# A hybrid decoder block on one core: small products in one run, the first norm from rows of x, x in four-tile pieces, its weights first, the last tile in pieces

## The chip, the core and the metric

The kernel runs on one core of one Trainium2 chip. Its engines are TensorE (PE; PEld is its weight load), VectorE (DVE), ScalarE (ACT), GpSimd (POOL) and SyncE (SP), and each works through its own list of instructions in order. DMAs are issued by an instruction of SP or of ACT. The metric is the device time of one launch in microseconds (us), the median of three runs.

## The reference, cut to what matters

One decoder layer over 256 tokens of width 2048, all in float32:

```python
h = rmsnorm(x, attn_norm_w)                      # x * rsqrt(mean(x*x) + EPS) * w
proj = h @ w_in                                  # 2048 -> 4*1024 + 3*1024 + 2*2048
rq, rk, rv, rg, mq, mk, mv, g_ret, g_moba = split(proj)
o_ret = silu(rg) * groupnorm(retention(rotary(rq), rotary(rk), rv)) * ret_norm_w   # 4 heads of 256
o_moba = causal softmax attention(rotary(mq), rotary(mk), mv)  # 8 heads of 128; 256 tokens are one block
merged = sigmoid(g_ret) * (o_ret @ w_ret_up) + sigmoid(g_moba) * (o_moba @ w_moba_up)
x = x + merged @ w_out
h2 = rmsnorm(x, ffn_norm_w)
a, b = split(causal_dwconv(h2 @ w_ffn_up, conv_w, conv_b))    # 2048 -> 2 * 5632
x = x + (silu(a) * b) @ w_ffn_down                            # 5632 -> 2048
return rmsnorm(x, final_norm_w)
```

## The kernel before

All weights stand in device memory as one stream of *halves*: a half is a tile of 128 x 1024 floats (512 KB), two k tiles (of 128 rows) by 512 columns. Two halves make a *slot*; a *group* is 512 columns of a product, and a group over 2048 rows takes four slots. `plan` lists the groups: values, then keys and queries of the MoBA heads, the same of the retention heads, gates, up-projections, `w_out`, then the feed-forward. Groups of keys and queries use weights as the stationary operand and products of 128x256; values, gates and most others have tokens stationary and products of 128x512.

Every float32 operand is split into a high and a low part: ACT copies `raw` to `whi` (line 131), DVE subtracts to get `wlo` (line 132), and `mm3` (line 142) makes three products, high by high, high by low, low by high. So a half can be multiplied by high parts alone when `whi` is there, and its second product needs `wlo`. `part(n)` splits half n, frees its raw buffer and loads half n + 4 (four raw buffers, four pairs of split buffers). `split2` with a scale (lines 134 and 135) does the same for a k tile of x: `xh` and `xl` in `xb`, times the norm's weight of that row, which lies in `vec`. The other factor of the first norm, r1 = rsqrt(mean of x squared), is the same for a whole token and is multiplied in after the products.

The set-up loads x transposed (`xT`, 16 k tiles of 128 x 256, two in a DMA) through four buffers, alternating with halves on SP's list. `part_x` (line 244) splits two k tiles at a time and, one step behind, squares the two before them on ACT (`sq`, `sqk`, lines 255 and 258) and adds them up on POOL (line 259). `setup` (line 263) is a task: with each slot it goes on to its next `yield`. It loads the constants, sums the squares over partitions by small products with a column of ones (`ss`, line 283), takes the root (POOL, line 186), spreads r1 over partitions (`across`) and scales the rotation tables with it.

Other tasks (one per head or group, started by `closed`) do attention, retention, gates, residuals and activations in stages, one stage a slot: a stage's ACT and DVE work stands behind the splits of the next slot's halves. Their small products on PE (`s`, `pt`, `o` of MoBA, `rs`, `ro`, `tr` of retention, `ftr` transposes) go into a list `between`; the slot's main products (`acc`) go into `stream`. `issue` (line 150) puts them on PE's list: main products in order, and from a third of the slot on, small ones spread evenly among them.

The last slot and the one before it run token tile by token tile, and `finish` (line 512) ends each: the residual is added (DVE, 518), squared with its sum (ACT, 519), the four partial sums are added (520), the root is taken (184, 186), the last 512 columns are multiplied by the final weight (522), and four pieces of 512 columns are scaled and stored, even ones by DVE and SP, odd ones by ACT and its own DMA queue.

Of the kernel before, what the change touches and what calls it, by code (L numbers as in the profile page):

```python
# [17 lines left out]
P = 128  # L18
# [62 lines left out]
def block(ctx: ExitStack, tc: tile.TileContext, a):  # L81
# [21 lines left out]
    n_halves = wts.shape[0]  # L103

    def spans(n):
        step = CW if n < 2 else 2 * CW
        return [slice(c, c + step) for c in range(0, 2 * CW, step)]

    def load(n, *some):
# [39 lines left out]

    def issue():  # L150

        n, m = len(stream), len(between)
        first, done = n // 3, 0
        for i, one_mm in enumerate(stream):
            one_mm()
            while done < m and done * (n - first) < (i + 1 - first) * m:
                between[done]()
                done += 1
        assert done == m
        stream.clear()  # L160
        between.clear()

# [50 lines left out]
                tasks.remove(g)  # L213

    vec = sb.tile([P, NVEC], F32, name="vec")
    nc.scalar.dma_start(vec[:, :V_RET], a["vec"][:, :V_RET])
    ident = sb.tile([P, P], F32, name="ident")
    one = sb.tile([P, 1], F32, name="one")
    nc.gpsimd.memset(one, 1.0)
# [11 lines left out]

    xts = {}

    def load_x(k):
        xts[k] = p0.tile([P, 2, S], F32, name="xt", bufs=RAW_BUFS)
        if k:
            nc.sync.dma_start(xts[k], a["xT"][:, k:k + 2, :])  # L237
            load(k // 2) if k < 2 * RAW_BUFS else None
        else:
            for j in range(2):  # L240
                nc.sync.dma_start(xts[0][:, j, :], a["xT"][:, j, :])
                load(0, spans(0)[j])

    def part_x(k):
        if k < KD:
            for j in range(2):
                split2(xh[:, k + j, :], xl[:, k + j, :], xts[k][:, j, :], vec[:, V_ATTN + k + j:V_ATTN + k + j + 1])
                if k == 0:
                    part(0, spans(0)[j])
        k -= 2  # L250
        if 0 <= k < KD:
            t = xts.pop(k)
            if k == 0:
                k1["sq"] = p0.tile([P, 2, S], F32, name="sq")
                nc.scalar.activation(k1["sq"], t, AF.Square)
            else:
# [3 lines left out]
            if k + 2 * RAW_BUFS < KD:  # L260
                load_x(k + 2 * RAW_BUFS)

    def setup():

        yield
        cst = {}
        nc.sync.dma_start(ident, a["ident"])
        for name, p in (("mask", P), ("rcos", P), ("rsin", P), ("mcos", P), ("msin", 32)):
            cst[name] = p0.tile([p, a[name].shape[1]], F32, name=name)
            nc.sync.dma_start(cst[name], a[name])  # L270
        k1["decay"] = p1.tile([P, RH, S], F32, name="decay")
        nc.sync.dma_start(k1["decay"], a["decay"])
        nc.sync.dma_start(vec[:, V_RET:], a["vec"][:, V_RET:])
        yield
        yield
        yield
        for name, src in (("one", ident), ("mask", cst["mask"])):
            k1[name] = p1.tile([P, P], BF16, name=name + "b")
            nc.scalar.activation(k1[name], src, AF.Copy)
# [4 lines left out]
        yield  # L284
# [9 lines left out]
        nc.vector.tensor_mul(k1["rsin"][:, 1, :], cst["rsin"], b)  # L294

    def keep_v(acc, vh, vl):
        for t in range(NT):
# [213 lines left out]

    def finish(acc, t):

        c = D // CW - 1
        w = slice(c * CW, (c + 1) * CW)
        x3 = big["x2"][:, t, :]
        ss = sb.tile([P, 1], F32, name="ss3t", bufs=2)
        nc.vector.tensor_add(x3[:, w], acc, x3[:, w])
        nc.scalar.activation(acc, x3[:, w], AF.Square, accum_out=big["ss3"][:, t, c:c + 1])
        nc.vector.reduce_sum(ss, big["ss3"][:, t, :], axis=AX.X)  # L520
        r = rsqrt("r3", ss, D)
        nc.vector.tensor_mul(x3[:, w], x3[:, w], big["wf"][:, w])
        for c in range(D // CW):
            w = slice(c * CW, (c + 1) * CW)
            if c % 2:
                nc.scalar.activation(x3[:, w], x3[:, w], AF.Copy, scale=r)  # L526
                nc.scalar.dma_start(orows[:, t, w], x3[:, w])
            else:
                nc.vector.tensor_scalar_mul(x3[:, w], x3[:, w], r)
                nc.sync.dma_start(orows[:, t, w], x3[:, w])  # L530


    now = {}
# [32 lines left out]
    def closed(kind, n, acc, more):  # L566
# [17 lines left out]
        elif kind == "wo":  # L584
            if n == 0:
                assert not tasks, len(tasks)
                right.close()
                pr = pool(right, "pr", "right")
                big["x2"] = pr.tile([P, NT, D], F32, name="x2")
                for k in ("ss2", "ss3"):  # L590
                    big[k] = sb.tile([P, NT, 4], F32, name=k)
# [24 lines left out]
    for n in range(RAW_BUFS):  # L616
        load_x(2 * n)
# [136 lines left out]
```

## Time and profile before

| | |
|---|---|
| median of three runs | 1456.74 us (1455.98 to 1457.03) |
| profiled execution, its own time | 1456.43 us |
| its span, first to last instruction | 1454.6 us |
| PE busy | 1440.2 us, 99% of the span |
| DVE, ACT, POOL busy | 895.2, 708.1, 58.9 us |
| mean granted TensorE clock | 0.998 of full speed |
| moved by DMA | 274.19 MB, mean 188 GB/s |

A row of a timeline reads: start, duration, engine, line, operation, tile written and tiles read, count; in brackets, how long the engine had been idle and what ended that. Rows of one kind that follow each other are merged, and "x2" then spans both. The chain of waits follows the end of the program back to its beginning: at each step to what released it. A window's row gives busy time and count for each engine, then granted clock, busy share of the DMA engines and GB/s.

### The profile page before, as it was taken

How to read it: one execution, taken by the hardware profiler on the slowest of the kernel's cores; microseconds unless marked ns; L12 is line 12 of the kernel's file. 1: busy time of each engine (PE TensorE's matmuls, PEld its weight loads, DVE VectorE, ACT ScalarE, POOL GpSimd, SP SyncE). 2: the span in 40 equal slices, each digit the busy share in tenths (PEclk: the TensorE clock that was granted, in tenths of full speed). 3: DMA queues.
4: the chain of work that ended last, by engine and by line, in shares of the span. 5: the costliest groups of instructions: out<-in, count | busy, mean ns of one | idle time of the engine just before them, and what ended most of it. 6: DMA issues, size and time to landing. Idle time of an engine off the chain costs nothing.

```text
span 1454.6 us, 20207 instructions
## 1 busy us (share of the span) xinstructions
PE 1440.2 (99%) x7910; PEld 1247.0 (86%) x7910; DVE 895.2 (62%) x1114; ACT 708.1 (49%) x933; POOL 58.9 (4%) x45
## 2 busy tenths in 40 slices
PE   8999999999999999999999999999999999999997
PEld 6989889899888888888898888888888888888886
DVE  7666655656554545455567777777777776445453
ACT  6444453444444444444455555555555555444343
POOL 3120200101000000000000000000000000000000
PEclk9999999999999999999999999999999999999999
DMA  8654545555555555566655555555555556555553
GB/s 281 203 174 160 166 162 182 175 186 172 175 188 189 189 191 188 198 217 192 201 188 188 188 189 189 189 188 189 188 189 188 188 189 217 195 195 190 195 194 116
DMA packets 77840, 274.19 MB, mean 188 GB/s; under 512 B 8720, under 2 KB 9776, under 8 KB 77616
## 3 DMA queue, kind: packets, MB, share of 16 engines
q1 hardware_dynamic: 77024, 271.84, 57.3%
q8 instruction: 62, 1.02, 0.3%
q10 hardware_dynamic: 720, 1.06, 0.2%
q14 instruction: 34, 0.28, 0.1%
HBM read 270.77 MB, written 2.10 MB: 188 GB/s over the span
## 4 chain that ended last, share of the span: by engine, by line
PE 97%; issue 1%; DVE 1%; DMA 1%; SPq 0%; ACT 0%; POOLq 0%; POOL 0%; ACTq 0%; DVEq 0%
PE acc L140 95%; DMA raw<-in_wts 1%; PE ftr L148 0%; PE s L140 0%; DVE xb L135 0%; PE o L140 0%; PE rs L140 0%; PE ro L140 0%; DVE wlo L132 0%; PE pt L148 0%; SPq L114 0%; PE tr L148 0%; ACT x L526 0%; SPq L237 0%; POOLq L750 0%
## 5 line engine op out<-in xcount | busy, mean ns | idle before, releaser
L132 DVE TENSOR_TENSOR wlo<-raw,whi 128x1024 fp32r<-128x1024 f32 (+1 forms) x506 | 625.9, 1238 | 526.6 <-ACT whi L131 525.8
L131 ACT ACTIVATE whi<-raw 128x1024 fp32r<-128x1024 f32 (+1 forms) x506 | 534.2, 1057 | 701.6 <-PE acc L140 594.5
L140 PE MATMUL acc<-xb,whi 128*128 128x512 f32 (+1 forms) x2496 | 551.3, 343 | 0.0
L140 PEld LDWEIGHTS acc<-xb,whi 128*128 128x128 f32 x2496 | 423.1, 190 | 43.5
L140 PE MATMUL acc<-xb,wlo 128*128 128x256 f32 x1920 | 352.1, 283 | 0.0
L140 PEld LDWEIGHTS acc<-xb,wlo 128*128 128x128 f32 x1920 | 293.6, 191 | 13.1
L140 PE MATMUL acc<-whi,xb 128*128 128x512 f32 x896 | 289.2, 397 | 0.5 <-ACT whi L131 0.4
L140 PEld LDWEIGHTS acc<-whi,xb 128*128 128x128 f32 x896 | 164.5, 188 | 34.9 <-ACT whi L131 1.6
L140 PE MATMUL acc<-wlo,xb 128*128 128x512 f32 x448 | 177.9, 397 | 3.5 <-DVE wlo L132 3.5
L140 PEld LDWEIGHTS acc<-wlo,xb 128*128 128x128 f32 x448 | 84.2, 188 | 23.0 <-DVE wlo L132 6.5
L140 PE MATMUL acc<-whi,gh 128*128 128x512 f32 x224 | 87.1, 389 | 0.0
L140 PE MATMUL acc<-wlo,gh 128*128 128x512 f32 x224 | 87.1, 389 | 0.0
L140 PE MATMUL acc<-whi,gl 128*128 128x512 f32 x224 | 87.1, 389 | 0.0
L494 DVE SCALAR_TENSOR_TENSOR y<-u,vec,y 128x256 f32<-128x256 f32 x176 | 73.3, 479 | 0.0
L140 PE MATMUL acc<-whi,mgh 128*128 128x512 f32 x128 | 50.9, 398 | 0.0
L140 PE MATMUL acc<-whi,mgl 128*128 128x512 f32 x128 | 50.9, 397 | 0.0
L140 PE MATMUL acc<-wlo,mgh 128*128 128x512 f32 x128 | 50.6, 395 | 0.0
L140 PE MATMUL acc<-whi,otmh 128*128 128x512 f32 x128 | 50.0, 391 | 0.0
L140 PE MATMUL acc<-whi,otml 128*128 128x512 f32 x128 | 49.9, 390 | 0.0
L140 PE MATMUL acc<-wlo,otmh 128*128 128x512 f32 x128 | 49.9, 390 | 0.0
L140 PE MATMUL acc<-whi,otrh 128*128 128x512 f32 x128 | 49.8, 389 | 0.0
L140 PE MATMUL acc<-wlo,otrh 128*128 128x512 f32 x128 | 49.8, 389 | 0.0
(157 smaller groups left out, 1028.7 us busy)
## 6 DMA issues: line engine op xcount, KB each, us to landing
raw<-in_wts SPq DMA_DIRECT2D x502, 512.0 KB, 4.0
xp<-in_x SPq DMA_DIRECT2D x4, 512.0 KB, 6.5
xt<-in_xT SPq DMA_DIRECT2D x7, 256.0 KB, 5.7
raw<-in_wts SPq DMA_DIRECT2D x4, 256.0 KB, 4.4
wf<-in_wf SPq DMA_DIRECT2D x1, 1024.0 KB, 8.1
out<-x SPq DMA_DIRECT2D x4, 256.0 KB, 3.1
out<-x ACTq DMA_DIRECT2D x4, 256.0 KB, 3.3
decay<-in_decay SPq DMA_DIRECT2D x1, 512.0 KB, 4.9
```

The source lines that it names most:

```text
L131: nc.scalar.activation(hi, full, AF.Copy)
L132: nc.vector.tensor_sub(lo, full, f32(hi))
L140: to.append(lambda: nc.tensor.matmul(out, a, b, **kw))
L494: nc.vector.scalar_tensor_tensor(y[:, j, :], u[:, j, i:i + S], cv[j][:, i:i + 1], y[:, j, :], op0=OP.mult, op1=OP.add)
```

## The change

There are five edits, and the code that goes with them.

1. `issue` puts all small products of a slot in one run at the middle of the slot's main products.
2. The first norm's sums come from x in rows (256 tokens by 2048): four tiles of 128 x 1024 are loaded on ACT's queue into the buffers that held the transposed x, squared on ACT with their sums, and added on DVE. The squares of the transposed tiles, POOL's sums and the `ss` products are gone. The stages of `setup` are spread over more slots, and its constants come later.
3. x lies in four buffers of four k tiles, all of it at once: two DMAs of 256 KB, then three of 512 KB. Half 1 comes whole and not in two pieces.
4. The norm's weights come on ACT's queue before anything else there (as before, though now in the code behind the idle products); a copy of one element makes ACT load its table at once.
5. `finish` takes the partial sums of the first three column groups ahead of the end, adds and squares the last 512 columns in two pieces of 256, and stores 3 x 448 columns by DVE and SP and 704 by ACT.

```diff
     def spans(n):
-        step = CW if n < 2 else 2 * CW
+        step = CW if n < 1 else 2 * CW
...
     def issue():
-        n, m = len(stream), len(between)
-        first, done = n // 3, 0
-        for i, one_mm in enumerate(stream):
+        middle = len(stream) // 2
+        for one_mm in stream[:middle] + between + stream[middle:]:
             one_mm()
-            while done < m and done * (n - first) < (i + 1 - first) * m:
-                between[done]()
-                done += 1
...
+    def load_x(k, n=4):
+        if k % 4 == 0:
+            xts[k // 4] = p0.tile([P, 4, S], F32, name="xt", bufs=4)
+        nc.sync.dma_start(xts[k // 4][:, k % 4:k % 4 + n, :], a["xT"][:, k:k + n, :])
     def part_x(k):
+        for j in range(k, min(k + 2, KD)):
+            split2(xh[:, j, :], xl[:, j, :], xts[j // 4][:, j % 4, :], vec[:, V_ATTN + j:V_ATTN + j + 1])
             if k == 0:
-                k1["sq"] = p0.tile([P, 2, S], F32, name="sq")
-                nc.scalar.activation(k1["sq"], t, AF.Square)
-            else:
-                sq = p1.tile([P, 2, S], F32, name="sqk", tag="full", bufs=2)
-                nc.scalar.activation(sq, t, AF.Square)
-                nc.gpsimd.tensor_add(k1["sq"], k1["sq"], sq)
+                part(0, spans(0)[j])
     def setup():
...
+        yield
+        yield
+        yield
+        sums = p0.tile([P, NT, 2], F32, name="sums")
+        rows = []
+        for i in range(4):
+            rows.append(p0.tile([P, D // 2], F32, name="rows", tag="xt", bufs=4))
+            nc.scalar.dma_start(rows[i], xrows[:, i // 2, (i % 2) * D // 2:(i % 2 + 1) * D // 2])
         nc.sync.dma_start(ident, a["ident"])
+        fetch("mask")
+        yield
+        fetch("rcos", "rsin", "mcos", "msin")
+        yield
...
-        ss = att("ss")
-        for t in range(NT):
-            for i in range(2):
-                mm(ss[:, t:t + 1], k1["sq"][:, i, t * P:(t + 1) * P], one, start=i == 0, stop=i == 1)
-        yield
-        k1["r1"] = rsqrt("r1", ss[:, :NT], D)
+        for i in range(4):
+            nc.scalar.activation(rows[i], rows[i], AF.Square, accum_out=sums[:, i // 2, i % 2:i % 2 + 1])
+            if i == 1:
+                yield
+        ss = p0.tile([P, NT], F32, name="ss")
+        nc.vector.reduce_sum(ss, sums, axis=AX.X)
+        k1["r1"] = rsqrt("r1", ss, D)
         yield
         b = across(k1["r1"])
...
     def finish(acc, t):
...
+        nc.vector.reduce_sum(ms[:, 2:], big["ss3"][:, t, :c], axis=AX.X)
+        nc.vector.tensor_scalar(ms[:, 0:1], ms[:, 2:], 1.0 / D, EPS, op0=OP.mult, op1=OP.add)
+        for i, v in enumerate(pieces):
+            nc.vector.tensor_add(x3[:, v], acc[:, i * half:(i + 1) * half], x3[:, v])
+        for i, v in enumerate(pieces):
+            sq = sb.tile([P, half], F32, name="sq3", bufs=2)
+            nc.scalar.activation(sq, x3[:, v], AF.Square, accum_out=big["ss3"][:, t, c + i:c + i + 1])
+            nc.vector.scalar_tensor_tensor(ms[:, i + 1:i + 2], big["ss3"][:, t, c + i:c + i + 1], 1.0 / D,
+                                           ms[:, i:i + 1], op0=OP.mult, op1=OP.add)
+        nc.gpsimd.tensor_tensor(r, ms[:, 2:], mhalf[:, :1], op=OP.pow)
         nc.vector.tensor_mul(x3[:, w], x3[:, w], big["wf"][:, w])
+        step = 448
+        for b in range(0, 3 * step, step):
+            w = slice(b, b + step)
+            nc.vector.tensor_scalar_mul(x3[:, w], x3[:, w], r)
+            nc.sync.dma_start(orows[:, t, w], x3[:, w])
+        w = slice(3 * step, D)
+        nc.scalar.activation(x3[:, w], x3[:, w], AF.Copy, scale=r)
+        nc.scalar.dma_start(orows[:, t, w], x3[:, w])
...
+    nc.scalar.dma_start(vec[:, :V_RET], a["vec"][:, :V_RET])
+    nc.scalar.activation(early, early, AF.Copy)
+    load_x(0, 2)
+    load(0)
+    load_x(2, 2)
+    load(1)
+    load_x(4)
+    load(2)
+    load(3)
+    load_x(8)
     part_x(0)
     part_x(2)
     part(1)
+    load_x(12)
     spawn(setup)
```

What moves can be seen on three stretches of the engines' lists. First, ACT at the start of the program, before (the splits of x, `xb`, and of the halves, `whi`, with the squares between them):

```order
L134 ACT_TABLE_LOAD
L134 ACTIVATE xb<-xt,vec 128x256
L131 ACTIVATE whi<-raw 128x512
L134 ACTIVATE xb<-xt,vec 128x256 x2
L255 ACTIVATE sq<-xt 128x512
L131 ACTIVATE whi<-raw 128x512 x2
L134 ACTIVATE xb<-xt,vec 128x256 x2
L258 ACTIVATE sqk<-xt 128x512
L131 ACTIVATE whi<-raw 128x1024
```

and the same stretch now:

```order
L616 ACT_TABLE_LOAD
L616 ACTIVATE early<-early 128x1
L134 ACTIVATE xb<-xt,vec 128x256
L131 ACTIVATE whi<-raw 128x512
L134 ACTIVATE xb<-xt,vec 128x256 x2
L131 ACTIVATE whi<-raw 128x1024
```

The squares between the splits are gone, and half 1 is split in one instruction. Second, ACT now in slots 3 to 7, where the rows of x are loaded and squared (`rows`, with `sums`), and the values' split `vh` takes r1 as its scale:

```order
L257 DMA rows<-in_x 128x1024 x4
L131 ACTIVATE whi<-raw 128x1024 x4
L265 ACTIVATE oneb<-ident 128x128
L265 ACTIVATE maskb<-mask 128x128
L267 ACTIVATE rows,sums<-rows 128x1024 x2
L131 ACTIVATE whi<-raw 128x1024 x2
L267 ACTIVATE rows,sums<-rows 128x1024 x2
L134 ACTIVATE vh<-acc,r_475 128x512 x2
L131 ACTIVATE whi<-raw 128x1024 x6
```

Before, only the two copies and four `whi` stood between the set-up and `vh`; the four squares have moved here from the first slots, and the second pair stands right ahead of the first reader of r1. Third, PE in slot 10, the first with the scores `s` of a MoBA head, before:

```order
L140 MATMUL s<-mh 128x128
L140 MATMUL acc<-xb,wlo 128x256
L140 MATMUL acc<-xb,whi 128x256 x2
L140 MATMUL acc<-xb,wlo 128x256
L140 MATMUL s<-ml,mh 128x128
L140 MATMUL acc<-xb,whi 128x256 x2
L140 MATMUL acc<-xb,wlo 128x256
L140 MATMUL acc<-xb,whi 128x256
L140 MATMUL s<-mh,ml 128x128
```

and now:

```order
L140 MATMUL acc<-xb,wlo 128x256
L140 MATMUL s<-mh 128x128
L140 MATMUL s<-ml,mh 128x128
L140 MATMUL s<-mh,ml 128x128
L140 LDWEIGHTS oneb
L140 MATMUL s<-maskb,oneb 128x128
L140 MATMUL s<-mh 128x256
L140 MATMUL s<-ml,mh 128x256
L140 MATMUL s<-mh,ml 128x256
L140 MATMUL acc<-xb,whi 128x256 x2
```

The eight products of the head now stand behind each other, with main products only ahead of the run and behind it. In the whole program 304 small products stand in 40 runs: 135 of 128 columns and 75 of 256 in 27 runs among main products of 512 columns, 61 and 33 in 13 runs among main products of 256.

## Rows read from the trace of the kernel before

**Rows 1.** The chain of waits, whole program: start, duration, what, count.

```profile
5.56 7.97 DMA raw<-in_wts
...
50.62 21.12 PE acc L140 x176
...
500.60 62.13 PE acc L140 x274
...
729.18 710.79 PE acc L140 x3783
```

**Rows 2.** Windows for products into `acc` alone, from the first to the 97th.

```profile
5.44:33.70 28.26, 24.61 (x97) 17.58 (x97) 0.00 (x0) 0.00 (x0) 1.00 0.84 292
```

**Rows 3.** Timeline of PE in the first stage.

```profile
14.23 0.50 PE L140 MATMUL acc<-wlo,xb 128*128 128x512 f32 x1 [1.01 <-DVE wlo L132]
...
28.33 0.50 PE L140 MATMUL acc<-wlo,xb 128*128 128x512 f32 x1 [1.00 <-DVE wlo L132]
```

**Rows 4.** Timeline of DVE in the first stage.

```profile
18.97 1.21 DVE L132 TENSOR_TENSOR wlo<-raw,whi 128x1024 fp32r<-128x1024 f32 x1
20.11 1.91 DVE L135 SCALAR_TENSOR_TENSOR xb<-xt,vec,xb 128x256 fp32r<-128x256 f32 x2
21.94 2.32 DVE L132 TENSOR_TENSOR wlo<-raw,whi 128x1024 fp32r<-128x1024 f32 x1
...
28.20 0.87 DVE L135 SCALAR_TENSOR_TENSOR xb<-xt,vec,xb 128x256 fp32r<-128x256 f32 x2
```

**Rows 5.** Timeline of POOL in the first stage.

```profile
21.61 1.57 POOL L259 TENSOR_TENSOR sq<-sq,sqk 128x512 f32<-128x512 f32 x1 [0.27 <-ACT sqk L258]
```

**Rows 6.** Timeline of ACT at the start.

```profile
6.37 0.63 ACT L131 ACTIVATE whi<-raw 128x512 fp32r<-128x512 f32 x1 [0.58 <-DMA raw<-in_wts]
...
10.30 0.91 ACT L134 ACTIVATE xb<-xt,vec 128x256 fp32r<-128x256 f32 x2 [0.77 <-DMA xt<-in_xT]
...
13.90 1.04 ACT L131 ACTIVATE whi<-raw 128x1024 fp32r<-128x1024 f32 x1
```

**Rows 7.** Windows of the first 14 us, all engines.

```profile
0.00:5.60 5.60, 4.01 (x11) 3.02 (x11) 0.94 (x3) 2.52 (x4) 0.34 (x6) 1.00 0.59 187
5.60:9.00 3.40, 3.18 (x12) 1.93 (x12) 2.39 (x5) 2.77 (x7) 0.00 (x0) 1.00 0.95 288
9.00:14.00 5.00, 3.88 (x14) 2.36 (x13) 3.47 (x5) 4.23 (x10) 1.29 (x1) 1.00 1.03 410
```

**Rows 8.** Timeline of ACT in slot 6.

```profile
49.16 0.69 ACT L134 ACTIVATE vh<-acc,r 128x512 fp32r<-128x512 f32 x1 [1.38 <-DVE vl L135]
```

**Rows 9.** The chain of waits from 35 to 75 us.

```profile
35.89 0.12 PE ss L140 x2
36.01 1.06 PE acc L140 x8
...
71.73 0.06 PE s L140
71.79 0.53 PE acc L140 x4
```

**Rows 10.** The chain of waits from 425 to 440 us.

```profile
430.21 0.11 PE ftr L148
...
434.34 5.68 PE acc L140 x25
```

**Rows 11.** Timeline of all engines behind the last product.

```profile
1446.17 0.60 ACT L519 ACTIVATE acc<-x 128x512 f32<-128x512 f32 x1 [1.43 <-DVE x L518]
...
1447.34 0.93 POOL L186 TENSOR_TENSOR r<-r3ms,mhalf 128x1 f32<-128x1 f32 x1 [4.51 <-DVE r3ms L184]
...
1448.31 0.88 DVE L529 TENSOR_SCALAR x<-x,r 128x512 f32<-128x512 f32 x2 [0.45 <-POOL r L186]
1448.82 0.81 SPq L530 DMA_DIRECT2D out<-x  x2
```

**Rows 12.** Windows at the end, all engines.

```profile
1450.00:1452.00 2.00, 0.00 (x0) 0.00 (x0) 0.00 (x0) 0.17 (x1) 0.00 (x0) 0.50 1.07 342
```

More of the change, by code (lines that the diff above doesn't have):

```diff
@@ L215, in block @@
     vec = sb.tile([P, NVEC], F32, name="vec")
-    nc.scalar.dma_start(vec[:, :V_RET], a["vec"][:, :V_RET])
     ident = sb.tile([P, P], F32, name="ident")
-    one = sb.tile([P, 1], F32, name="one")
-    nc.gpsimd.memset(one, 1.0)
+    early = sb.tile([P, 1], F32, name="early")
+    nc.gpsimd.memset(early, 1.0)
     mhalf = sb.tile([P, NT], F32, name="mhalf")
@@ L232, in block, with fetch @@
     xts = {}
[L234 to L238, printed above, removed]
-        else:
-            for j in range(2):
-                nc.sync.dma_start(xts[0][:, j, :], a["xT"][:, j, :])
-                load(0, spans(0)[j])
-    def part_x(k):
[L245 to L252, printed above, removed]
-            if k == 0:
-                k1["sq"] = p0.tile([P, 2, S], F32, name="sq")
-                nc.scalar.activation(k1["sq"], t, AF.Square)
-            else:
-                sq = p1.tile([P, 2, S], F32, name="sqk", tag="full", bufs=2)
-                nc.scalar.activation(sq, t, AF.Square)
-                nc.gpsimd.tensor_add(k1["sq"], k1["sq"], sq)
-            if k + 2 * RAW_BUFS < KD:
-                load_x(k + 2 * RAW_BUFS)
+    def load_x(k, n=4):
+        if k % 4 == 0:
+            xts[k // 4] = p0.tile([P, 4, S], F32, name="xt", bufs=4)
+        nc.sync.dma_start(xts[k // 4][:, k % 4:k % 4 + n, :], a["xT"][:, k:k + n, :])
+    def part_x(k):
+        for j in range(k, min(k + 2, KD)):
+            split2(xh[:, j, :], xl[:, j, :], xts[j // 4][:, j % 4, :], vec[:, V_ATTN + j:V_ATTN + j + 1])
+            if k == 0:
+                part(0, spans(0)[j])
     def setup():
-        yield
         cst = {}
[L267 to L273, printed above, removed]
+        def fetch(*names):
+            for name in names:
+                p = a[name].shape[0]
+                cst[name] = p0.tile([p, a[name].shape[1]], F32, name=name)
+                nc.sync.dma_start(cst[name], a[name])
         yield
@@ L276, in setup @@
         yield
[L277 to L285 removed]
+        sums = p0.tile([P, NT, 2], F32, name="sums")
[3 more added lines that the diff above has]
+            nc.scalar.dma_start(rows[i], xrows[:, i // 2, (i % 2) * D // 2:(i % 2 + 1) * D // 2])
+        nc.sync.dma_start(ident, a["ident"])
+        fetch("mask")
+        yield
+        fetch("rcos", "rsin", "mcos", "msin")
+        yield
+        for name, source in (("one", ident), ("mask", cst["mask"])):
+            k1[name] = p1.tile([P, P], BF16, name=name + "b")
+            nc.scalar.activation(k1[name], source, AF.Copy)
+        for i in range(4):
[5 more added lines that the diff above has]
+        k1["r1"] = rsqrt("r1", ss, D)
         yield
@@ L294, in setup @@
         nc.vector.tensor_mul(k1["rsin"][:, 1, :], cst["rsin"], b)
+        yield
+        k1["decay"] = p1.tile([P, RH, S], F32, name="decay")
+        nc.sync.dma_start(k1["decay"], a["decay"])
+        nc.sync.dma_start(vec[:, V_RET:], a["vec"][:, V_RET:])
     def keep_v(acc, vh, vl):
@@ L512, in finish @@
     def finish(acc, t):
-        c = D // CW - 1
+        c, half = D // CW - 1, CW // 2
         w = slice(c * CW, (c + 1) * CW)
         x3 = big["x2"][:, t, :]
[L517 to L521, printed above, removed]
-        nc.vector.tensor_mul(x3[:, w], x3[:, w], big["wf"][:, w])
[L523 to L530, printed above, removed]
+        ms = sb.tile([P, 3], F32, name="r3ms", bufs=2)
+        r = sb.tile([P, 1], F32, name="r3", bufs=2)
+        nc.vector.reduce_sum(ms[:, 2:], big["ss3"][:, t, :c], axis=AX.X)
+        nc.vector.tensor_scalar(ms[:, 0:1], ms[:, 2:], 1.0 / D, EPS, op0=OP.mult, op1=OP.add)
+        pieces = [slice(c * CW + i * half, c * CW + (i + 1) * half) for i in range(2)]
+        for i, v in enumerate(pieces):
[6 more added lines that the diff above has]
+        nc.gpsimd.tensor_tensor(r, ms[:, 2:], mhalf[:, :1], op=OP.pow)
+        nc.vector.tensor_mul(x3[:, w], x3[:, w], big["wf"][:, w])
+        step = 448
[6 more added lines that the diff above has]
+        nc.scalar.dma_start(orows[:, t, w], x3[:, w])
     now = {}
@@ L590, in closed @@
                 for k in ("ss2", "ss3"):
-                    big[k] = sb.tile([P, NT, 4], F32, name=k)
+                    big[k] = sb.tile([P, NT, 4 + (k == "ss3")], F32, name=k)
             spawn(residual, acc, now["xp"], n)
@@ L614, in block @@
         nc.tensor.matmul(t[:, :S], idle[:, 0, :P], idle[:, 0, :], start=True, stop=True)
-    for n in range(RAW_BUFS):
-        load_x(2 * n)
+    nc.scalar.dma_start(vec[:, :V_RET], a["vec"][:, :V_RET])
[8 more added lines that the diff above has]
+    load_x(8)
     part_x(0)
```

1 line of the change is left out of this document (removed).

## Prediction

> **What bounds the kernel now.** I read the chain of waits first. It is PE nearly all the way: from 729 us to 1440 us one unbroken line of main products, before that main products with small ones between them, and in front of all that a stretch of DMA, DVE and ACT [rows 1]. So there are only three places where time can be won: the first stage, the small products, and what follows the last product. A product of 512 columns costs 62.13/274 = 0.2268 us in that line and one of 256 columns 21.12/176 = 0.12 us [rows 1].
>
> The windows on `acc` give the first stage its size. Its 96 products (the row counts the next one too) run from 5.44 to 33.70 us, 28.26 us, where 96 x 0.2268 = 21.8 would do [rows 2]. So 6.5 us are stops. The PE timeline names them: a second product of a half waits about 1 us for DVE's `wlo`, first at 14.23, last at 28.33 [rows 3]. DVE's own timeline shows why: where POOL is idle a `wlo` takes 1.21 and the low parts of two k tiles 0.87; beside POOL's addition of squares, such as the one at 21.61, they take 2.32 and 1.91 [rows 4, 5]. The undisturbed work of a half is 1.21 + 0.87 = 2.08 us on DVE and 1.04 + 0.91 = 1.95 on ACT [rows 4, 6], both under the 12 x 0.2268 = 2.72 that PE needs; disturbed it is over that.
>
> **Transposed squares out, x in four tiles, half 1 whole (edits 2 to 4, first stage).** With POOL's seven additions gone nothing in DVE's way is left, and behind the opening PE should run without a stop. The opening is set by the DMAs. The windows give about 1.05 MB moved by 5.6 us, then 288 GB/s to 9 us and 410 to 14 us [rows 7]. Against them I lay three landings. The second piece of half 0 is the 0.79th MB in SP's order and would be through at about 4.7; ACT had it at 6.37. The tiles of x for half 2 are the 1.84th MB, 8.3 by the windows, and ACT had them at 10.30 [rows 6]. Half 3 is the 3.15th MB, 11.7 by the windows, and landed at 5.56 + 7.97 = 13.53 [rows 1]. So a piece lands 1.7 to 2.0 us after its last byte's turn in issue order.
>
> In the new order x tiles 0 and 1, half 0, x tiles 2 and 3 are again the first 1.05 MB, done at 5.6. Half 1 follows, 0.52 MB: through at 6.9 (at 410 GB/s) or 7.4 (at 288), landed at 8.7 to 9.3. It is now one ACT instruction of 1.04 and one DVE instruction of 1.21, so its second product comes at about 11.1 to 11.7, later than in two pieces. Eleven more products (2.5 us) bring PE to 13.6 to 14.2. Half 2 has 0.52 MB of x and itself ahead: through at 9.5 to 11, landed at 11.3 to 12.9, its `wlo` done 2.25 later, at 13.6 to 15.2. So the second product of half 2, at 14.23 before, stands between 13.6 and 15.2. I take 14.1, since x now also comes in pieces of 4 KB per partition as the stretch with 410 GB/s mostly had them. From there 71 products at 0.2268 make 16.1 us: the stage ends at 30.2 instead of 33.70, a gain of 3.5 (2.4 to 4.0 by the two ends). That ACT loads its table early, and that the first piece of x is twice as large, moves the first product by some tenths and nothing behind half 1.
>
> The `ss` products: two passes take 0.12, and eight main products behind them 1.06 instead of 0.96, so each costs 0.22 [rows 9]; four are gone: 0.9.
>
> What comes instead is four loads of 512 KB on ACT's queue in slot 3 and four squares of 128x1024 in slots 5 and 6, which I put at 1.04 to 1.3 each from the split of that size [rows 6]. They cost nothing as long as ACT and DVE stay ahead of PE. Slot 3 begins at about 24.8; 2.1 MB take 5 us at 410 GB/s plus 2 to land, so the rows are there by 34 or 35, and the first square, behind slot 5's splits, is not due before 37. The narrow place is slot 6. PE enters it at 30.2 + 2 x 48 x 0.12 = 41.7. ACT then splits its second half until 42.8, squares until 45.3; DVE's sums 0.3 and POOL's root 0.93 [rows 11] give r1 at 46.6; behind it stand `vh` 0.69, a wait of 1.38 for DVE and `vh` again [rows 8], to 49.4, and only then the split of slot 8's first half, whose low part is ready at about 51.7. PE enters slot 8 at 53.2. So 1.5 us are spare; a delay beyond that goes one to one into the end.
>
> **One run of small products (edit 1).** Among main products of 256 columns a small one of 128 costs 0.06 + 0.53 - 4 x 0.12 = 0.11 [rows 9]: its own columns take 0.06, and the main product behind it is late by 0.05. Among products of 512 columns, eight transposes and the 14 main products between them take 434.34 - 430.21 = 4.13 us, up to the product behind the last [rows 10], so a transpose costs (4.13 - 14 x 0.2268)/8 = 0.12. In a run the neighbour is another small one. I take 0.11 for it there, the price it has among short neighbours, and 0.12 for one of 256 columns, the pace of such products among themselves. Then 135 small ones save 0.01 each, the 75 wider ones perhaps as much, less something at the ends of 27 runs; the other 94 save nothing. I put down 1.3 us. From below, if changing between kinds at the ends costs more than it saves: -1.5. From above the price of the bare columns, 0.06, which is the second rival.
>
> The Trainium skill, "TensorE: Matmul & The Clock Gate", section LDWEIGHTS (loading the stationary operand), has a weight load last its columns over 1.2 GHz, 107 ns for 128, whatever is multiplied. That speaks against a large gain from a run; the 0.11 and 0.12 of the rows agree with it, and by it this term would be 1.9 and the sum 1449.8.
>
> A run needs all its inputs at the middle of the slot, where before only its first third did. I cost that at nothing: a stage reads what ACT and DVE made in the slot before, and the chain passes from main to small product and back without a gap [rows 9, 10].
>
> **The last tile (edit 5).** Square, sum, root and scaling follow each other [rows 11]. The addition in two pieces lets the first square start sooner, and of the two small DVE steps ahead of the root one is left: I take 0.2 off, and 0.05 for DVE's first store piece of 448 columns instead of 512 (0.44). But behind the first store the DMA engines are full: 342 GB/s from 1450 to 1452 [rows 12], and 1.05 MB at that rate take 3.1 us. The end therefore follows the first store (issued at 1448.82), not the last [rows 11]: 0.3, at least 0, at most 0.8 if the last store, which now is issued some 0.8 earlier, counts.
>
> **The sum.** 3.5 + 0.9 + 1.3 + 0.3 = 6.0 us off the profiled execution's own 1456.43 (span 1454.6): 1450.4. The median of the runs shown is 1456.74, 0.3 above it, so the same gain from there is 1450.7; I keep 1450.4.
>
> **The rivals.**
>
> *The opening stays late.* Half 1 waits as a whole, and if the larger pieces of x around it delay it (landing at 11.5), the second product of half 2 comes at 17 and the stage ends at 33.1. PE then stands still for some 3 us with few products between. At the end of the program the granted clock is at 0.50, 1.2 GHz, in 1450 to 1452 [rows 12], and PE had stopped before the square at 1446.17 [rows 11]; the windows up to 14 us have 1.00 with stops of 1 us [rows 7]. A clock at half costs 0.2268 us for each product of 512 columns made under it. Start gain 0.6, sum 3.1: 1453.3. For it: the landings above are scattered by some tenths and all late. Against it: the bytes ahead of half 1 are the same as before.
>
> *A run goes at the pace of its columns.* 128 columns at 0.06 instead of 0.115, 196 products: 10.8 in place of 1.3, which gives 1440.9. For it: the product behind a small one does start 0.06 after it. Against it: it then takes 0.05 longer, so two together are no faster. The Trainium skill, "TensorE: Matmul & The Clock Gate", section Back-to-back issue gap, has 81 ns for a stream of products of 128 columns, which would give 196 x 0.034 = 6.7 and 1445.0; no run of such products stands in this trace.
>
> *Slower: the run waits.* If ACT or DVE is late with the last input of a run, all of PE waits at the middle of the slot, where before other main products stood between. The other three terms give 4.7, so it decides from 4.7/40 = 0.12 us a run; at 0.25 a run it is 10 - 4.7 = 5.3 above: 1461.7. For it: PE executes in order, and the run brings the last small ones forward by up to half a slot. Against it: the inputs are a slot old, and DVE is busy for only 895 of the 1454.6 us. The late r1 is the same case at one place; it needs 1.5 + 6 us of delay.
>
> **Chances.** Forecast, 1447.5 to 1453: 0.74; late opening: 0.13; faster runs: 0.06; waits that eat the gain or more: 0.07. 0.2% of the time, 2.9 us, is about what a measurement tells from no change. Faster: the forecast, the faster runs and half of the late opening, 0.86; same: the other half and some of the waits, 0.09; slower 0.05. The range holds the forecast with its ends and most of the late opening: 1447.2 to 1453.6.
>
> **What would show it.** Right: the first stage without waits for `wlo` behind half 2, its end near 30.2; DVE's pairs at 0.87 throughout; no idle time of PE before a run; runs with 0.11 from one small product to the next; `wlo` of slot 8 ahead of PE; the last square's end about 0.2 nearer to the last product. Wrong: PE waiting at the middle of slots, a half-1 landing after 10, a clock below 1.00 before the end, runs at 0.06 to 0.08.

## The result, and the profile after

The changed kernel takes 1449.49 us (median of six runs, 1448.49 to 1450.74) against 1457.0 for the kernel before (1455.98 to 1457.37): ratio 0.9949, 95% interval 0.9939 to 0.9959. The profiled execution took 1449.64 us, its span 1447.4 instead of 1454.6. I divide the 7.2 us at three points of the two traces: the first product of 256 columns (33.70 in [rows 2], now 30.53: 3.17 gained), the start of the last tile's addition (DVE's line 518, at 1445.44 in the timeline of before; now line 514, at 1439.21: 3.06 more), and the end of the span (0.97 more).

The chain of waits, whole program after (start, duration, what, count):

```profile
9.21 1.06 ACT whi L131
10.29 1.24 DVE wlo L132
11.57 39.27 PE acc L140 x251
```

In [rows 1] a stretch of DMA, DVE and ACT ran to 28 us; now PE is the chain from 11.57 on. PE's timeline in the first stage has two waits that are left, both for half 1:

```profile
10.31 0.51 PE L140 MATMUL acc<-whi,xb 128*128 128x512 f32 x1 [0.95 <-ACT whi L131]
11.57 0.50 PE L140 MATMUL acc<-wlo,xb 128*128 128x512 f32 x1 [0.75 <-DVE wlo L132]
```

DVE's timeline, which answers to [rows 4]:

```profile
20.41 0.87 DVE L135 SCALAR_TENSOR_TENSOR xb<-xt,vec,xb 128x256 fp32r<-128x256 f32 x2
21.74 1.23 DVE L132 TENSOR_TENSOR wlo<-raw,whi 128x1024 fp32r<-128x1024 f32 x1 [0.45 <-ACT whi L131]
```

The 1.91 and 2.32 of before are gone, and now DVE waits for ACT. The runs in the chain of waits, 60 to 75 and 424 to 430 us, answer to [rows 9, 10]:

```profile
68.56 0.84 PE s L140 x8
...
425.17 0.87 PE ftr L148 x8
```

Eight transposes in a row take 0.87, 0.109 each; no wait of PE stands before a run. Behind the last product (timeline of all engines, against [rows 11]):

```profile
1440.85 0.94 POOL L520 TENSOR_TENSOR r<-r3ms,mhalf 128x1 f32<-128x1 f32 x1 [4.51 <-DVE r3ms L518]
1441.82 0.88 ACT L528 ACTIVATE x<-x,r 128x704 f32<-128x704 f32 x1 [1.24 <-POOL r L520]
1441.82 1.18 DVE L525 TENSOR_SCALAR x<-x,r 128x448 f32<-128x448 f32 x3 [0.45 <-POOL r L520]
1442.30 1.33 SPq L526 DMA_DIRECT2D out<-x  x3
1442.73 0.37 ACTq L529 DMA_DIRECT2D out<-x  x1
```

From the addition to the end of the root it is 2.58 us (2.83 before: [rows 11] with the addition's start above), and the issue of the last store ends at 1443.63, 1.84 behind the root.

One place looks quite different from what was forecast. ACT's timeline where the rows of x are loaded, then DVE's and PE's:

```profile
25.30 8.48 ACTq L257 DMA_DIRECT2D rows<-in_x  x4
33.89 2.95 ACT L131 ACTIVATE whi<-raw 128x1024 fp32r<-128x1024 f32 x3 [7.53 <-PE acc L140]
```

```profile
34.98 3.50 DVE L132 TENSOR_TENSOR wlo<-raw,whi 128x1024 fp32r<-128x1024 f32 x3 [7.37 <-ACT whi L131]
```

```profile
36.29 0.40 PE L140 MATMUL acc<-xb,whi 128*128 128x256 f32 x2
36.53 0.28 PE L140 MATMUL acc<-xb,wlo 128*128 128x256 f32 x1
```

Four loads held ACT for 8.48 us: the first three were out by 28.4, the fourth went at 33.45. What ACT waited for stands in the semaphore events of the trace. A semaphore here is a counter by which a transfer tells that it has landed; this program uses eight of them in turn for the transfers of both queues, and the fourth load has the one of a half that SP had issued at 24.92. ACT waited until that half had landed, at 33.37. The split behind the loads was done at 34.95, its `wlo` at about 36.2, and the product that reads it stood at 36.53: nothing was lost, with 0.3 us to spare. The last of the rows landed at 39.97, where the prediction had 34 or 35; the squares, from 40.40 on, did not wait for it.

### The profile page after: what moved, and what is told of

The parts are those of the page before. It is cut to its first block, busy times and chain, and to the rows that moved or that the text cites. A ratio compares the mean times of both kernels' runs of the same rounds, so it can differ in the third digit from the quotient of the medians.

```text
span 1447.4 us, 20173 instructions
## 1 busy us (share of the span) xinstructions
PE 1436.3 (99%) x7902; PEld 1252.5 (87%) x7902; DVE 888.8 (61%) x1122; ACT 707.5 (49%) x935; POOL 49.2 (3%) x38
## 3 DMA queue, kind: packets, MB, share of 16 engines
q10 hardware_dynamic: 1008, 2.83, 0.5%
## 4 chain that ended last, share of the span: by engine, by line
PE 98%; DMA 0%; issue 0%; DVE 0%; ACT 0%; SPq 0%; POOLq 0%; POOL 0%; DVEq 0%
PE acc L140 96%; PE ftr L148 0%; PE s L140 0%; DMA raw<-in_wts 0%; PE rs L140 0%; PE o L140 0%; PE ro L140 0%; PE pt L148 0%; PE tr L148 0%; DVE wlo L132 0%; ACT whi L131 0%; POOLq L758 0%; POOL r L520 0%; ACT sq L517 0%; PE across L140 0%
## 5 line engine op out<-in xcount | busy, mean ns | idle before, releaser
L140 PE MATMUL acc<-xb,whi 128*128 128x512 f32 (+1 forms) x2496 | 545.5, 342 | 0.0
L140 PE MATMUL acc<-whi,xb 128*128 128x512 f32 x896 | 283.5, 392 | 0.9 <-ACT whi L131 0.9
L140 PEld LDWEIGHTS acc<-whi,xb 128*128 128x128 f32 x896 | 168.8, 188 | 36.0 <-ACT whi L131 1.8
```

Of the source, the lines that this page charges most:

```text
L140: to.append(lambda: nc.tensor.matmul(out, a, b, **kw))
```

## The experiments

Twelve kernels ran, in three groups, each beside the kernel before on the same chip (medians of 1456.71 to 1456.96 there). Where a trace's end is compared, I use the time from the stage's end (first product of 256 columns) to the end of the span, since the opening varies from one execution to the next: five profiles of the same opening have 30.53, 29.97, 30.38, 29.77 and 30.16, and three profiles of the kernel before's opening have 33.70, 34.47 and 34.64.

**1. Runs alone.** Kernel before, with `issue` of the changed kernel:

```diff
...
-            while done < m and done * (n - first) < (i + 1 - first) * m:
...
+        for one_mm in stream[:middle] + between + stream[middle:]:
```

> The kernel before with edit 1 alone. Theory: a run takes each small product down to 0.107 to 0.11 us from 0.12 to 0.135, in the middle of the program, and does nothing at its two ends: 1457.0 - 2.2 = 1454.8 us (1454.5 to 1455.2), first stage still ending near 33.7. Rival A, the 0.01 a product that the prediction used: 1455.7. Rival B, the gain in the middle came from something else in the change (fewer stops of ACT or DVE): 1457.0. Rival C, a product of 128 columns at 0.081 in a run: about 1450.3.

Measured 1454.82 against 1456.71, ratio 0.9987 (0.9979 to 0.9996): 1.9 us off. From the stage's end (34.47) to the end of the span (1453.3) it is 1418.8, before 1420.9: 2.1. So the gain in the middle of the program beyond the `ss` products comes from the runs. The chain of waits of this kernel, 35 to 75 us, also prices the `ss` products, which it still has:

```profile
37.51 0.79 PE ss L140 x8
```

The 3.06 us of the middle are these 0.8, the 2.1 of the runs, and 0.2 that lies within the readings.

Where the 2.1 lie can be read too, since the traces of both kernels have the same 7584 main products in the same order. I compare their starts from the twelfth main product ahead of a run to the twelfth behind it, and from the 24th to the 24th among products of 256 columns. Over the 27 runs among products of 512 columns (210 small products) the kernel before takes 2.0 us longer; over the 13 runs among products of 256 columns it takes 0.1 less.

**2 and 3. Each transpose twice,** in the changed kernel (run) and in the kernel before (spread):

```diff
-        between.append(lambda: nc.tensor.transpose(out, full, ident))
+        for _ in range(2):
+            between.append(lambda: nc.tensor.transpose(out, full, ident))
```

> The changed kernel with each of its 104 transposes made twice, the second behind the first into the same place: it prices a small product in a run by itself. Theory, 0.109 each: + 11.3, so 1449.5 + 11.3 = 1460.8 us. Rival at 0.081: 1457.9. Rival at the pace of the columns, 0.06: 1455.7. Rival at the spread price of 0.12 or more: 1462.0 or more.

> The kernel before (small products spread) with each of its 104 transposes made twice. Theory, 0.121 to 0.136 each among products of 512 columns: + 12.6 to 14.1, so 1469.6 to 1471.1 us. Rival, a small product costs the same spread as in a run (0.109): + 11.3, 1468.3.

Measured 1460.43 and 1469.19. In the run that is 10.9 above 1449.49, and by the traces (1458.2 - 29.97 against 1447.4 - 30.53) 11.36, or 0.109 for each of the 104. Spread it is 12.5 above the kernel before, and by the traces (1467.7 - 34.64 against 1454.6 - 33.70) 12.16, or 0.117. The theory of the run holds; my range for spread ones, from 0.121, was too high. The chain of waits of the spread kernel shows where the difference lies:

```profile
435.82 0.24 PE acc L140
436.06 0.11 PE ftr L149
436.17 0.24 PE acc L140
436.40 0.11 PE ftr L149
```

A transpose and the main product behind it take 0.345 together; without the 0.2268 of a main product among its own kind 0.118 is left. A run saves 0.008 to 0.009 for a transpose among products of 512 columns, and neither 0.081 nor 0.06 is its price. The Trainium skill, "TensorE: Matmul & The Clock Gate", section LDWEIGHTS (loading the stationary operand), has the time of a weight load go by its columns alone, 107 ns for 128; the 0.109 in the run agrees with it.

**4. No additions on POOL** in the kernel before (its first norm then leaves out the squares of 14 of the 16 k tiles):

```diff
-                nc.gpsimd.tensor_add(k1["sq"], k1["sq"], sq)
```

> The kernel before without POOL's seven additions of squares (the first norm then sums the squares of two k tiles only); the squares on ACT, the order of the loads and the buffers of x stay. Theory, POOL's additions alone hold DVE up: DVE's wlo takes 1.21 and a pair 0.87 throughout, the stage ends at 30.5 to 31.2 instead of 33.70, the time is 1453.8 to 1454.5 us. Rival, ACT's squares or the order of the loads are the cause: the stage still ends at 33 or later, 1456.5 or more.

Measured 1454.01, ratio 0.9982 (0.9973 to 0.9991): 2.7 off, and the stage ends at 31.12 instead of 33.70. DVE's timeline has no long row left, with the old loads, the old buffers and ACT's squares all in place:

```profile
21.04 1.23 DVE L132 TENSOR_TENSOR wlo<-raw,whi 128x1024 fp32r<-128x1024 f32 x1 [0.25 <-ACT whi L131]
22.19 0.88 DVE L135 SCALAR_TENSOR_TENSOR xb<-xt,vec,xb 128x256 fp32r<-128x256 f32 x2
```

**5 and 6. One of the two back in the changed kernel:** seven additions on POOL, or eight squares on ACT, results read by nobody:

```diff
+            nc.gpsimd.tensor_add(k1["dummy"], t, t)                     # 5: t = high parts of two k tiles
+            nc.scalar.activation(k1["dummy"], xts[...][...], AF.Square)   # 6
```

> The changed kernel with seven dummy additions of 128x512 on POOL in the first stage, each behind ACT's split of a pair of k tiles, its result read by nobody. Theory: DVE's wlo and pairs beside an addition take about 2.3 and 1.9 again, PE waits for wlo again, the stage ends at 32.5 to 33.7 instead of 30.53, the time is 1451.5 to 1452.7 us. Rival, the new loads and the squares gone from ACT made the gain: 1449.5, stage end 30.5.

> The changed kernel with eight dummy squares of 128x512 on ACT in the first stage, where the kernel before had them, and nothing on POOL. Theory: 0.62 more a half, 2.57 in all on ACT against PE's 2.72, is hidden: stage end 30.5 to 30.9, time 1449.4 to 1449.9 us. Rival, ACT's squares were part of the stops: stage end 31.5 or later, 1450.5 or more.

The additions alone gave 1450.16, 0.7 above the changed kernel and less than half of what I expected; the stage ended at 30.84, 0.3 later, though its half 1 had come 0.6 earlier. So my theory that POOL's additions make the stops whatever is beside them fell. DVE's timeline of experiment 5 shows why:

```profile
15.13 2.06 DVE L132 TENSOR_TENSOR wlo<-raw,whi 128x1024 fp32r<-128x1024 f32 x1
...
21.41 1.21 DVE L132 TENSOR_TENSOR wlo<-raw,whi 128x1024 fp32r<-128x1024 f32 x1
22.54 1.65 DVE L135 SCALAR_TENSOR_TENSOR xb<-xt,vec,xb 128x256 fp32r<-128x256 f32 x2
```

An addition that starts behind ACT's split of a pair mostly lies beside DVE's own pair and lengthens that, by 0.8; of the six `wlo` from half 1 on, five stay at 1.21 to 1.23. The one that was hit, at 15.13, is the only one behind half 1 that PE waited for (0.44 before 17.25). A half of 1.21 and 1.65 takes 2.86 on DVE against PE's 2.72, too little too much to add up to stops in six halves.

The squares alone gave 1449.36: hidden, as expected. But the profiled execution of this kernel was its slowest, 1450.92, and its stage ended at 31.79. The windows (PE, PEld, DVE, ACT and POOL busy, then granted clock, DMA share, GB/s) show something else than the squares:

```profile
11.00:12.00 1.00, 0.80 (x2) 0.63 (x3) 0.93 (x3) 1.00 (x2) 0.00 (x0) 0.74 1.04 426
12.00:13.00 1.00, 1.00 (x4) 0.80 (x3) 0.55 (x1) 1.00 (x3) 0.00 (x0) 0.50 1.04 426
13.00:14.00 1.00, 1.00 (x4) 0.81 (x3) 1.00 (x3) 1.00 (x3) 0.00 (x0) 0.50 1.02 418
```

PE had waited 0.95 before 9.94 and 0.76 before 11.20, much as it does for half 1 in the changed kernel (0.95 and 0.75), and here the granted clock then fell to 0.50, 1.2 GHz, until about 14.9; in the profile of the changed kernel it stayed at 1.00. From the second wait's end to the stage's end this profile has 20.59 us and that of the changed kernel 18.96: the drop cost 1.6.

**7. Half 1 in two pieces:**

```diff
-        step = CW if n < 1 else 2 * CW
+        step = CW if n < 2 else 2 * CW
```

> The changed kernel with half 1 in two pieces again (loaded and split as two of 128x512). Theory: the second product of half 1 comes sooner than 11.57, but half 2 sets the pace behind it, its wlo done at 14.07 where PE now comes at 14.3: at most 0.2 gained, 1449.2 to 1449.6 us, stage end 30.3 to 30.6. Rival, the whole half 1 costs the 1.7 us that PE waits for it: 1448.0 us, stage end 29.0 to 29.5.

Measured 1449.02 (1448.72 to 1449.17), stage end 29.95. That is 0.5 under the changed kernel's median, where I expected 0.2 at most, but inside the spread of its runs and profiles; the forecast of half 2 as the next to be late holds (PE waits 0.75 for its `wlo` at 13.73), so the rival with 1.7 does not.

**8. Rows loaded by SP:**

```diff
-            nc.scalar.dma_start(rows[i], xrows[...])
+            nc.sync.dma_start(rows[i], xrows[...])
```

> The changed kernel with the four loads of rows issued by SP instead of ACT. Theory: ACT is no longer held for 8 us by the issue, PE did not wait for it and gains nothing: 1449.3 to 1449.7 us; ACT's list has no gap of 7.5 us between 25 and 34. Rival A, ACT's stop was hidden only just and its removal shows in the stage that follows: 1448.5 to 1449.0. Rival B, the loads now stand ahead of the halves on SP's list and make PE wait: 1450.5 or more.

Measured 1449.28 (1448.64 to 1450.63): no difference. SP had the four loads out in 2.09 us, and ACT's splits follow PE again:

```profile
27.64 2.09 SPq L257 DMA_DIRECT2D rows<-in_x  x4
```

```profile
30.36 1.06 ACT L131 ACTIVATE whi<-raw 128x1024 fp32r<-128x1024 f32 x1 [1.66 <-PE acc L140]
```

On SP the fourth load had nothing to wait for: the half before it on its semaphore had landed at 24.08. So the 8.48 us of ACT were hidden in the changed kernel.

**9 and 10. The last tile:** `finish` as before; then the new additions, squares and sums with the old scaling and stores:

```diff
-        step = 448
-        for b in range(0, 3 * step, step):
...
+        for c in range(D // CW):          # four pieces of 512, even ones DVE and SP, odd ones ACT
...
```

> The changed kernel with the last tile as before (edit 5 undone). By the trace, from the start of the residual's addition to the end of the span it takes 9.16 us before and 8.19 after: 1449.5 + 1.0 = 1450.5 us, span from that addition to the end 9.1 to 9.2. Rival, the prediction's reading that the end follows the first store: 1449.8, 8.5. Rival, the tail's difference between the two traces is chance: 1449.5.

> The changed kernel with the new additions, squares and sums of the last tile, but its scaling and stores as before (four pieces of 512 columns, by DVE and ACT in turn). Theory: the end follows the last store, which in the old split is issued 0.7 later behind the root, while the root itself is only 0.25 earlier by the new sums: 1449.5 + 0.7 = 1450.2 us, 8.9 from the addition to the end. Rival, the end follows the first store: 1449.5, 8.2 to 8.3.

Measured 1450.41 and 1450.09: 0.9 and 0.6 above the changed kernel, with runs that overlap (1449.77 to 1451.77 and 1449.45 to 1451.54), so the traces have to tell. Behind the addition's start the spans have 9.02 (1438.48 to 1447.5) and 8.74 (1439.06 to 1447.8), against 8.19. So the new sums are worth 0.3 and the new stores 0.6. POOL's root and ACT's queue in experiment 10:

```profile
1440.69 0.93 POOL L520 TENSOR_TENSOR r<-r3ms,mhalf 128x1 f32<-128x1 f32 x1 [4.51 <-DVE r3ms L518]
...
1442.41 0.34 ACTq L526 DMA_DIRECT2D out<-x  x1
1442.80 0.72 ACT L525 ACTIVATE x<-x,r 128x512 f32<-128x512 f32 x1 [0.41 <-DVE x L528]
1443.55 0.34 ACTq L526 DMA_DIRECT2D out<-x  x1
```

The issue of the last store ends at 1443.89, 2.27 behind the root instead of 1.84. The windows with bytes and the one behind them (busy times as above, then clock, DMA share, GB/s), first of experiment 10, then of the changed kernel, whose root ends 0.17 later:

```profile
1443.00:1444.00 1.00, 0.00 (x0) 0.00 (x0) 0.00 (x0) 0.52 (x1) 0.00 (x0) 1.00 1.02 373
1444.00:1445.00 1.00, 0.00 (x0) 0.00 (x0) 0.00 (x0) 0.00 (x0) 0.00 (x0) 0.53 1.09 305
1445.00:1446.00 1.00, 0.00 (x0) 0.00 (x0) 0.00 (x0) 0.00 (x0) 0.00 (x0) 0.50 0.95 315
1446.00:1447.00 1.00, 0.00 (x0) 0.00 (x0) 0.00 (x0) 0.00 (x0) 0.00 (x0) 0.50 0.15 55
```

```profile
1443.00:1444.00 1.00, 0.00 (x0) 0.00 (x0) 0.00 (x0) 0.00 (x0) 0.00 (x0) 1.00 0.90 327
1444.00:1445.00 1.00, 0.00 (x0) 0.00 (x0) 0.00 (x0) 0.00 (x0) 0.00 (x0) 0.50 1.01 385
1445.00:1446.00 1.00, 0.00 (x0) 0.00 (x0) 0.00 (x0) 0.00 (x0) 0.00 (x0) 0.50 0.92 337
1446.00:1447.00 1.00, 0.00 (x0) 0.00 (x0) 0.00 (x0) 0.00 (x0) 0.00 (x0) 0.50 0.00 0
```

The measured times lie near those of the theory, but its reason, that the end follows the last store, is not shown. In both kernels the DMA engines are full from the first bytes to the last window but one, so they did not stand still for want of the last store. What differs is how long the same 1.05 MB kept them busy: by the sum of the shares 3.21 us in four pieces of 512 columns, 2.83 in 3 x 448 and 704. That is 0.4 of the 0.6. Whether the width of the pieces, their order or their division between the two queues makes it, no run here separates.

**11. Squares and additions both back** in the changed kernel, chained as the kernel before had them:

```diff
+                nc.scalar.activation(sq, t, AF.Square)
+                nc.gpsimd.tensor_add(k1["dummy"], k1["dummy"], sq)
```

> The changed kernel with the squares on ACT and POOL's seven additions of them back as the kernel before had them, their sum read by nobody; loads and buffers of x stay new. POOL's additions alone cost 0.3 to 0.7 here, the squares alone nothing but a drop of the clock in one profile, while the kernel before gained 2.7 without the additions. Theory, the two together make the stops, since an addition behind a square lies beside a wlo too, and both engines then lie above PE's 2.72 a half: stage end 32.7 to 33.7, 1451.7 to 1452.8 us. Rival, with the new loads the additions no longer matter: stage end 30.5 to 31.5, 1449.5 to 1450.5.

Measured 1453.64 (1453.04 to 1454.14), 4.15 above the changed kernel: more than the whole gain of the first stage. It lies 0.8 above my range. The stage ends at 33.14, 2.6 later. DVE's timeline has the long rows again, now beside POOL's:

```profile
12.10 1.72 DVE L132 TENSOR_TENSOR wlo<-raw,whi 128x1024 fp32r<-128x1024 f32 x1 [0.52 <-ACT whi L131]
13.74 1.90 DVE L135 SCALAR_TENSOR_TENSOR xb<-xt,vec,xb 128x256 fp32r<-128x256 f32 x2
...
16.70 2.95 DVE L135 SCALAR_TENSOR_TENSOR xb<-xt,vec,xb 128x256 fp32r<-128x256 f32 x2
```

```profile
13.53 1.43 POOL L249 TENSOR_TENSOR sq<-sq,sqk 128x512 f32<-128x512 f32 x1 [0.80 <-ACT sqk L248]
15.79 3.57 POOL L249 TENSOR_TENSOR sq<-sq,sqk 128x512 f32<-128x512 f32 x2 [0.83 <-ACT sqk L248]
```

The pair began at 13.74, and the addition ended at 14.96, 1.22 later; the pair took 1.03 longer than its 0.87. In [rows 4, 5] the `wlo` of 21.94 lay 1.24 beside an addition and took 1.11 longer. The Trainium skill, "SBUF — State Buffer", section Who interferes with whom, has a VectorE instruction with two inputs in SBUF contend with a GpSimd instruction that reads SBUF, over a pair of ports that is an exclusive lock. The rows agree with it: DVE is longer by nearly the time that it lies beside an addition. It can also be POOL that is longer. The `wlo` of 18.97 in [rows 4] took its 1.21 although an addition began beside it, and that addition took 2.00, where others of the same timeline took 1.30:

```profile
17.08 1.30 POOL L259 TENSOR_TENSOR sq<-sq,sqk 128x512 f32<-128x512 f32 x1 [1.34 <-ACT sqk L258]
19.34 2.00 POOL L259 TENSOR_TENSOR sq<-sq,sqk 128x512 f32<-128x512 f32 x1 [0.97 <-ACT sqk L258]
```

A pair that meets two additions in a row, as the one of 16.70, takes 2.95. From the `wlo` of 12.10 to that of 26.53, four halves on, DVE needs 3.6 us a half.

One count leaves the opening's variation out: from the second product of half 2, the last that the opening makes late, to the stage's end PE has 71 products to make.

| profile | in the first stage beside the splits | second product of half 2 | stage's end | between |
|---|---|---|---|---|
| before | squares and additions | 14.23 | 33.70 | 19.5 |
| experiments 1, 3 | squares and additions | 15.09, 15.26 | 34.47, 34.64 | 19.4, 19.4 |
| experiment 11 | squares and additions | 13.87 | 33.14 | 19.3 |
| experiment 5 | additions | 13.88 | 30.84 | 17.0 |
| experiment 4 | squares | 14.88 | 31.12 | 16.2 |
| experiment 6 | squares | 15.66 | 31.79 | 16.1 |
| changed kernel | nothing | 14.44 | 30.53 | 16.1 |
| experiments 2, 8, 9, 10 | nothing | 13.68 to 14.28 | 29.77 to 30.38 | 16.1 |

So squares and additions together cost 3.2 to 3.4 us, with the old loads and with the new; additions alone cost 0.9 and squares alone nothing. The additions of experiments 5 and 11 read different tiles (one tile twice; the running sum and a square), so whether the company of the squares or the tiles make the difference between 0.9 and 3.2 is not separated.

The other 1.2 us of the two spans come later, at a place the changed kernel passes with 0.3 to spare. PE's timeline of experiment 11:

```profile
40.26 0.39 PE L140 MATMUL acc<-xb,wlo 128*128 128x256 f32 x1 [0.76 <-DVE wlo L132]
```

Here the half on the fourth load's semaphore landed at 37.36, the load went at 37.45, ACT's next split began at 37.89, and its `wlo` was late: the product at 40.26 stands 1.1 behind the pace of the products ahead of it.

**12. A better version:** halves 1 and 2 both in two pieces (`n < 3` in the line of experiment 7).

> The changed kernel with halves 1 and 2 both in two pieces, as a better version: with half 1 in two pieces PE last stops for 0.75 at the second product of half 2 (13.73), where the wlo of half the size would be ready 0.5 to 1.1 earlier. Theory: 1448.3 to 1448.8 us, stage end 29.2 to 29.7, no run above 1450. Rival, the landings move with the pieces and the stop stays: 1449.0.

Measured 1448.03 (1447.62 to 1448.57), ratio 0.9938 (0.9926 to 0.9951), the best of all kernels here and a little better than I expected, 1.5 under the changed kernel's median, though the two ratios' intervals overlap. Its stage ends at 28.75, outside what the profiles of the other opening show, and PE's longest wait in it is 0.43. The second product of half 2 comes at 12.66, 1.8 earlier than in the changed kernel, and the 71 products behind it take 16.1 again. No run reached 1450; of the changed kernel's six one did, and five of the variants with the same opening had a run or two that lay more than 1 us above their median.

## Why the prediction was right

**First stage, 3.5 forecast, 3.17 measured.** The stop and its cause were right: without POOL's additions 2.7 us go (experiment 4), with them and ACT's squares back they return (experiment 11), and behind half 2 PE makes its 71 products in the 16.1 us of the forecast. What the prediction did not say is that the cost depends on how the additions fall: those of experiment 5 cost 0.9, the old ones 3.2 to 3.4. Its reading of [rows 4] as "where POOL is idle" does not hold for the `wlo` of 18.97, beside which an addition ran and was itself lengthened; the 1.21 is the undisturbed time all the same (experiment 4). Half 1's second product came at 11.57 (forecast 11.1 to 11.7), half 2's `wlo` was done at 14.07 (13.6 to 15.2), PE did not wait for it, and the end was 30.53 in this profile and 29.8 to 30.4 in others, forecast 30.2. The 3.17 is a lower end: the profile of before has the earliest of four old openings, with the second product of half 2 at 14.23, 14.88, 15.09 and 15.26, against 13.7 to 14.4 in seven of the new one. The means differ by 0.9, a gain that the prediction put at 0.1; which of the loads, the buffers, the whole half 1 and the early table makes it was not tested one by one. The rival of a late opening had the right price in the wrong place: a clock at 0.50 was seen in one profile of a kernel with this opening, and cost 1.6.

**`ss`, 0.9 forecast, 0.8 measured** (0.79 for the eight of experiment 1).

**Runs, 1.3 forecast, 2.1 measured.** The 0.01 for a small product among products of 512 columns was right, and so was "the other 94 save nothing": by experiment 1 the 210 among products of 512 columns save 2.0, 0.0096 each, and those among products of 256 columns lose 0.1. The step that was mis-sized is "less something at the ends of 27 runs": 135 and 75 times 0.01 make 2.1, and the 0.8 taken off for the ends is not there. (By the trace of the changed kernel 65, not 61, products of 128 columns stand among products of 256; that changes nothing here.) By the 107 ns of the Trainium skill's page named above the term was 1.9, nearer to it.

**Last tile, 0.3 forecast, 0.97 measured.** Root and sums gave 0.25 to 0.3, as forecast. What failed is the time behind the first store: the prediction let 1.05 MB take 3.1 us at the rate of [rows 12], whichever way they are divided, so that only the first store's time counted. With the same new sums the old division of the stores takes 0.6 longer (experiment 10), though its first store is issued only 0.03 later behind the root: 0.4 of it is the longer work of the DMA engines on the same bytes. Whether the last store's later issue makes the rest stays open. The row with 342 GB/s is a mean of 2 us; the windows of single us show where the stores ended.

**Rows of x, nothing forecast, nothing measured,** but for a reason that the prediction did not have. It gave issuing four loads no time; they held ACT for 8.48 us, until a half of SP's had landed. The narrow place it named, slot 6 with the split of slot 8's first half behind it, came out 2.0 us ahead of PE; the narrowest was the start of slot 5 with 0.3 us, and in experiment 11 that was gone.

The sum of the terms fell 1.2 short of the 7.2 in the span. What lies around the span was 1.8 us before and 2.2 after, so 0.8 of that shows in the execution's own time, 1449.64 against 1450.4. By the medians the gain is 7.5 us against 6.0: the profile of before, 0.6 under its kernel's median, hides part of the opening's gain. No term made up for another: none came out much below its forecast, and two came out above.

## What to carry to other kernels

Where two engines both lie just under the pace of a third, price an elementwise helper on POOL by what it does to DVE's instructions beside it, and test it together with the work that sets its place in time: alone it cost 0.7 us here, together with the squares 4.2. A load on an engine's list can hold that engine until a transfer of another queue has landed: put large loads on the list of an engine that nobody waits for, and look at what stands behind them. Where executions vary in the opening, count from the last product that the opening makes late. To read an end of stores, take windows of 1 us, and add up the DMA share besides looking for the last bytes.

## What the runs showed of the hardware that was not expected

From the first to the last issue of four loads of 512 KB ACT's queue took 3.2 to 10.3 us in nine kernels (3.70 in experiment 7, 8.48 in the changed kernel, 10.25 in experiment 11), SP's queue 2.09. In all nine it is the fourth that goes late, and in all nine it goes 0.08 to 0.10 us behind the landing of the half that had its semaphore before it: 28.01 and 28.08 in experiment 7, 33.37 and 33.45 in the changed kernel, 37.36 and 37.45 in experiment 11. So ACT was not busy with issuing; it waited for a transfer that SP had issued 4.3 to 8.5 us before that landing.

The second: two waits of PE of under 1 us each, 1.26 us apart from start to start, were followed by a granted clock of 0.50 for 3.4 us in one execution (experiment 6) and by none in the profile of the changed kernel, with the same code in front of them on PE. The two executions differ further ahead: in experiment 6 PE had also waited 0.18 and 0.23 us before its first two products of 512 columns, which took 0.50 each; in the changed kernel it had not, and they took 0.79 each.
